# Scores stacked through DRAM, and the attention gate moved onto weight tiles

## The chip, the cores and the metric

One core of a Trainium2 chip runs the kernel. The metric is the device time of one execution in microseconds (us). The engines are TensorE (PE in the rows; its weight loads are PEld), VectorE (DVE), ScalarE (ACT), GpSimd (POOL) and SyncE (SP, which only starts transfers).

## The reference, cut to what matters

Two layers of a diffusion backbone run on 256 latent and 256 context tokens of width 1024. In each, the modulated input is projected to three attention groups; their heads are joined and go through one output projection, whose result is multiplied by a gate of the conditioning before it is added to the stream; a gated convolutional feed-forward follows. The second layer gives only latent tokens out, so there only latent queries are computed.

```python
s = einsum('bhqcd,bhkcd->bhcqk', q, k) * scale      # A: 6 heads, 2 maps each, 32 dimensions
p = softmax(s); p = p[:, :, 0] - lam * p[:, :, 1]

s_win = q @ k_window * scale + bias, masked          # B: 6 heads of 64 dimensions, 8x16 window
p = softmax(concat(s_win, q @ k_ctx * scale))        #    and all context keys

mix = concat(o_a, o_b, o_c) @ w_out                  # C: 4 heads of 96 dimensions
x = layernorm(ALPHA * x + ga * mix) * g + b          # ga: the gate, one number a column
```

## The kernel before

Nearly all products run on numbers split in two, a high part that TensorE's float32r format holds and the rest: hi·hi + lo·hi + hi·lo, three matmuls for one (lines 134 to 136 add them up). ScalarE makes the high part (L121 for weights, L126 and L130 for activations), VectorE the low part by a subtraction (L122, L127, L131).

Tokens stand side by side, 512 columns in layer 0 (256 context, then 256 latent) and, for queries, 256 in layer 1. One projection `fm` gives 128 rows by up to 512 columns, from 24 matmuls. An A tile i holds two heads of two maps of 32 rows; a B tile two heads of 64 rows. Their splits lie in tiles `stq` and `stk`, planes hi and lo beside each other. `score3` (L622) makes a score bank of 128 queries by 256 or 512 keys from three matmuls on 32 rows (A) or 64 (B) of TensorE; it fills two banks in turn, the two maps of a head (A) or the two heads (B), each on its own rows. C's scores (L831) take 96 rows in plain float32, one matmul each. The softmax takes a maximum (L381) and a reciprocal (L385) on VectorE and an exponential on ScalarE (L384); in A the second map is scaled (L702) and joined with the first (L703); then p is transposed (L392) and multiplied with the values (L400). In B, GpSimd masks a bias (L743, L744) that VectorE adds to the score (L745).

The parts of a layer are written in the order of `ORDERS`: "aq1" projects the queries of A's tile 1, "bk2" the keys of B's tile 2, "A0" is the attention of A's tile 0, "W3" the early part of the output projection for one weight block. A list scheduler then sets the order of each engine's own queue when the program is built, from its own planned times; it interleaves projections with attention. Each engine works its queue strictly in that order. Score tiles are slots of a pool: nine "st" in layer 0, seven "stq" and eight "stk" in layer 1; a writer waits for the last reader of its slot.

Weights come by SyncE's transfers into four "raw" buffers. At the end of layer 1's attention the last block of the output projection is added, `gated` (L892) multiplies each of four sums of 128x512 by the gate row on VectorE (L897) and adds it to the stream (L898); normalisation (L318 to L344) and the feed-forward follow.

Of the kernel before, what the change touches and what calls it, by code (L numbers as in the profile page):

```python
# [8 lines left out]
F32 = mybir.dt.float32  # L9
F32R = mybir.dt.float32r  # L10
AF = mybir.ActivationFunctionType
ALU = mybir.AluOpType
# [13 lines left out]
A_SCALE = 32 ** -0.5  # L26
# [4 lines left out]
ROT = [16 * (i // 16) + (i % 16 + 8) % 16 for i in range(32)]  # L31


CORE = (("qf",), ("vm",), ("sq",), ("pT",), ("rpb",), ("p1",), ("rot",),
        ("cosk", "sink", "bones", "ones", "m01", "mneg"), ("st", "stq", "stk"), ("p0",), ("vt",))


# [40 lines left out]
def build(nc, tc, st, I, out):  # L78
    P = 128
# [23 lines left out]
    def scp():  # L103
        return bank("sc", 2)
# [4 lines left out]
    def load(dst, src):  # L109
        nc.sync.dma_start(out=dst, in_=src)  # L110
# [1 line left out]
    def wraw(n):  # L112
        return wp.tile([P, n], F32, tag="raw", name="raw", bufs=4)

    def wsplit(src, n, pl=None, tag="", bufs=3, ring=False):
        raw = pl.tile([P, n], F32, tag="raw" + tag, name="raw", bufs=1) if pl and bufs == 1 and not ring else wraw(n)
        load(raw, src)
        pl = pl or wp
        hi = pl.tile([P, n], F32R, tag="whi" + tag, name="whi", bufs=bufs)
        lo = pl.tile([P, n], F32R, tag="wlo" + tag, name="wlo", bufs=bufs)  # L120
        S.copy(hi, raw)  # L121
        V.tensor_tensor(lo, raw, hi.bitcast(F32), ALU.subtract)  # L122
        return hi, lo

    def split_from(src, hi, lo):
        S.copy(hi, src)  # L126
        V.tensor_tensor(lo, src, hi.bitcast(F32), ALU.subtract)  # L127

    def split_scaled(src, hi, lo, scale):
        S.mul(hi, src, scale)  # L130
        V.scalar_tensor_tensor(lo, src, scale, hi.bitcast(F32), ALU.mult, ALU.subtract)  # L131
# [157 lines left out]
    def gate_row(l, r, cond, j, slot):  # L289
        t = tmp.tile([P, 512], F32, tag=("bada", "adarow")[slot], name="gate", bufs=1)  # L290
        load(t, garow[l, r][cond, 512 * j:512 * j + 512].partition_broadcast(P))
        return t
# [243 lines left out]
    for l in range(L):  # L536
# [82 lines left out]
            pump(PF)  # L619
            return proj(w, [LAT, CTX] if cc["early"] and cols == ALL else [cols])  # L620

        def score3(banks, q, k, rows, r0, qs, nk):  # L622
            for t, (a, b) in enumerate(((0, 0), (0, 1), (1, 0))):
                for n, sc in enumerate(banks):
                    r = slice(r0 + rows * n, r0 + rows * n + rows)
                    T.matmul(sc[:, 0:nk], lhsT=q[r, a, qs], rhs=k[r, b, 0:nk], start=t == 0, stop=t == 2,  # L626
                             tile_position=(r.start, 0))

        def st_q(dt=F32R):
            return ap.tile([P, 2, nq], dt, tag="stq" if last else "st", name="stq", bufs=7 if last else 9)  # L630

        def st_k(dt=F32R):
            return ap.tile([P, 2, 512], dt, tag="stk" if last else "st", name="stk", bufs=8 if last else 9)
# [45 lines left out]
        def proj_aq(i):  # L679
            po = fm(i, qc)  # L680
            q = ap.tile([P, 512], F32, tag="qf", name="qf", bufs=2)
            rope(ap, q[:, LAT], po, 0, P, K["cosk"], K["sink"])
            if not last:
                S.copy(q[:, CTX], po[:, CTX])
            aqs[i] = st_q()
            split_scaled(q[:, qc], aqs[i][:, 0, :], aqs[i][:, 1, :], A_SCALE)

        def proj_ak(i):
            po = fm(3 + i, ALL)
            k = ap.tile([P, 512], F32, tag="qf", name="kf", bufs=2)  # L690
            rope(ap, k[:, LAT], po, 0, P, K["cosk"], K["sink"])
            S.copy(k[:, CTX], po[:, CTX])
            aks[i] = st_k()
            split_from(k, aks[i][:, 0, :], aks[i][:, 1, :])

        def attn_a(i):
            def sco(h, e, qs, qt, nk, name):
                banks = [scp() for _ in range(2)]
                score3(banks, aqs[i], aks[i], 32, 64 * e, qs, nk)
                (p0, s0), (p1, s1) = [softmax_rows(sc, nk, ap, f"p{m}") for m, sc in enumerate(banks)]  # L700
                V.tensor_tensor(s1[:, 1:2], s1[:, 1:2], lam[:, 2:3], ALU.mult)
                V.tensor_scalar_mul(p1[:, 0:nk], p1[:, 0:nk], s1[:, 1:2])  # L702
                V.scalar_tensor_tensor(p0[:, 0:nk], p0[:, 0:nk], s0[:, 1:2], p1[:, 0:nk], ALU.mult, ALU.add)  # L703
                return p0

            def fin(po, c):
                sq = ap.tile([P, 256], F32, tag="sq", name="sq", bufs=2)
                S.activation(sq, po, AF.Square)
                pm = tpp()
                T.matmul(pm[:, 0:256], lhsT=K["bones"], rhs=sq, start=True, stop=True)  # L710
                S.activation(sq, pm[:, 0:256], AF.Ln, bias=epsc)
                S.activation(sq, sq, AF.Exp, scale=-0.5)
                V.scalar_tensor_tensor(sq, po, nw[:, 0:1], sq, ALU.mult, ALU.mult)
                split_from(sq, mix[0][:, i, c], mix[1][:, i, c])

            heads(i, sco, vt, 0, fin)
# [2 lines left out]

        def proj_bq(i):  # L720
            po = fm(6 + i, qc)
            bqs[i] = st_q()
            split_scaled(po[:, qc], bqs[i][:, 0, :], bqs[i][:, 1, :], B_SCALE)

        def proj_bk(i):
            po = fm(9 + i, ALL)
            bks[i] = st_k()
            split_from(po, bks[i][:, 0, :], bks[i][:, 1, :])

        def attn_b(i):  # L730
            banks = []

            def sco(h, e, qs, qt, nk, name):
                if e == 0:
                    banks[:] = [scp() for _ in range(2)]
                    score3(banks, bqs[i], bks[i], 64, 0, qs, nk)
                sc = banks[e]
                if name == "lat":
                    bt = ap.tile([P, 256], F32, tag="rpb", name="rpb", bufs=3)
                    load(bt, I["rpb"][l, h, qt])  # L740
                    b3 = bt.rearrange("p (a c) -> p a c", c=64)
                    with tc.issue_after(hT["pow"]):
                        G.tensor_tensor(b3, b3, K["m01"].unsqueeze(1).to_broadcast([P, 4, 64]), ALU.mult)  # L743
                    G.tensor_tensor(b3, b3, K["mneg"].unsqueeze(1).to_broadcast([P, 4, 64]), ALU.add)  # L744
                    V.tensor_tensor(sc[:, LAT], sc[:, LAT], bt, ALU.add)  # L745
                return normed(sc, nk)

            heads(i, sco, vt, 416 if i else 384, simple_fin(3 + i))
# [88 lines left out]
            pend.extend([ada(l, "b"), ada(l, "c")])  # L837
        outp = {}
        odone = []

        def out_mm(po, t, jb, w, kk, done):
            j = 2 * jb + kk
# [3 lines left out]
                not done and kk == 0, len(done) == 3 and kk == 1)  # L846

        def out_early(jb):
            for hf in range(2 if last else 1):
                w = wsplit(I["w_out"][l, hf, jb], 1024)  # L850
                for t in toks:
                    if not odone:
                        outp[t, hf] = acc() if len(outp) < 3 else adap()
                for kk in range(2):
                    for t in toks:
                        out_mm(outp[t, hf], t, jb, w, kk, odone)
            odone.append(jb)
# [34 lines left out]
        def gated(gates, po, t, hf):  # L892
            c = slice(512 * hf, 512 * hf + 512)
            if hf == 0:
                rsum[t] = sm.tile([P, 4], F32, tag="rsum", name="rsum")
                V.memset(rsum[t][:, 3:4], 0.0)
            V.tensor_tensor(po, po, gates[1 if t < 2 else 0], ALU.mult)  # L897
            V.scalar_tensor_tensor(xr[t][:, c], xr[t][:, c], ALPHA, po, ALU.mult, ALU.add,  # L898
                                   accum_out=rsum[t][:, hf:hf + 1])

# [34 lines left out]
        def token_major(pl, rnd, name, order, act, off, wpl, nres, head, tail, allres=False, nkeep=0):  # L935
# [16 lines left out]
            if allres:  # L952
                rem = [jb for jb in order if jb not in odone]
                ws = {}
                for i, jb in enumerate(rem):
                    for hf in range(2):
                        ws[jb, hf] = wsplit(I[name][l, hf, jb], 1024, wpl if i else None, f"r{hf}" if i else "", 1 if i else 3,
                                            True)
                gts = [gate_row(l, rnd, 0, hf, hf) for hf in range(2)]
                for t in toks:  # L960
                    for i, jb in enumerate(rem):
                        for hf in range(2):
                            for kk in range(2):
                                out_mm(outp[t, hf], t, jb, ws[jb, hf], kk, odone + rem[:i])
                            if i == len(rem) - 1:
                                gated([gts[hf]], outp[t, hf], t, hf)
                    head(t)
                tail(toks)
                return
# [310 lines left out]
```

## Time and profile before

| | us |
|---|---|
| median of 3 runs (1155.33 to 1157.75) | 1156.91 |
| profiled execution, its own time | 1158.58 |
| its span, first to last instruction | 1156.5 |
| TensorE busy in the span | 1107.0 |
| VectorE busy | 836.1 |
| ScalarE busy | 591.2 |
| GpSimd busy | 83.8 |

The mean granted clock of TensorE was 0.986 of full speed. A busy time counts an engine's instructions; matmuls are pipelined, so the duration of one is longer than the step from one to the next. The chain of waits, followed back from the end, tells that step. The profile's chain lies on TensorE for 85% of the span.

### The profile page before, as it was taken

The numbers are of one execution on the slowest core, as the hardware profiler recorded it, in microseconds if no ns is written. First come the engines' busy times: TensorE is split into PE (matmuls) and PEld (weight loads), VectorE is DVE, ScalarE is ACT, GpSimd is POOL, SyncE is SP. The second block draws the span as 40 slices with busy tenths as digits, with TensorE's granted clock in tenths as the row PEclk, the third lists the DMA queues.
The fourth block names the chain that finished last, engine by engine and source line by source line (L and its number), as shares of the span: only waits on it lengthen the run. The fifth ranks groups of instructions, "written<-read, shape, count | busy, mean of one in ns | idle before, by whom it ended". The sixth has DMA issues, their size and how long they took to land.

```text
span 1156.5 us, 17907 instructions
## 1 busy us (share of the span) xinstructions
PE 1107.0 (96%) x6776; PEld 902.1 (78%) x6776; DVE 836.1 (72%) x1505; ACT 591.2 (51%) x1063; POOL 83.8 (7%) x104
## 2 busy tenths in 40 slices
PE   5999999999998999999999999999999979999997
PEld 3877666686778888887888877897778758999985
DVE  4544677757588887986977687666766777888755
ACT  4345556656548644444352245555555656666541
POOL 0000100003123000000000002110000420000000
PEclk9999999999999999999999999998999988999999
DMA  9767112112143554643558894533111333555662
GB/s 362 295 241 279 58 37 74 37 37 86 51 164 97 197 169 144 199 152 116 186 174 309 311 328 131 176 94 99 53 55 56 128 132 121 183 183 188 201 203 89
DMA packets 58213, 179.19 MB, mean 155 GB/s; under 512 B 7024, under 2 KB 12432, under 8 KB 58128
## 3 DMA queue, kind: packets, MB, share of 16 engines
q1 hardware_dynamic: 58128, 178.05, 45.8%
q8 instruction: 54, 0.88, 0.3%
q14 instruction: 31, 0.25, 0.1%
HBM read 176.94 MB, written 1.08 MB: 154 GB/s over the span
## 4 chain that ended last, share of the span: by engine, by line
PE 85%; DVE 6%; ACT 2%; issue 2%; POOL 2%; DMA 2%; SPq 0%; DVEq 0%; POOLq 0%; ACTq 0%
PE acc L134 21%; PE acc L135 21%; PE acc L136 21%; PE sc L626 6%; PE tp L392 3%; PE tp L400 3%; PE sc L831 2%; DVE wlo L122 1%; PE sc L134 1%; PE sc L135 1%; PE sc L136 1%; POOL xn L344 1%; DMA rawr<-in_w_ada_e 1%; PE ada L234 1%; PE ada L136 1%
## 5 line engine op out<-in xcount | busy, mean ns | idle before, releaser
L121 ACT CAST whi<-raw 128x1024 fp32r<-128x1024 f32 (+3 forms) x204 | 212.0, 1043 | 248.7 <-PE acc L135 124.4
L122 DVE TENSOR_TENSOR wlo<-raw,whi 128x1024 fp32r<-128x1024 f32 (+3 forms) x204 | 248.4, 1221 | 121.4 <-ACT whi L121 117.1
L134 PE MATMUL acc<-hhi,whi 128*128 128x256 f32 (+1 forms) x960 | 327.3, 341 | 3.5 <-ACT hhi L360 3.5
L135 PE MATMUL acc<-hlo,whi 128*128 128x256 f32 (+1 forms) x960 | 325.4, 339 | 0.5 <-DVE hlo L361 0.3
L136 PE MATMUL acc<-hhi,wlo 128*128 128x256 f32 (+1 forms) x960 | 324.1, 338 | 0.4 <-DVE wlo L122 0.4
L134 PEld LDWEIGHTS acc<-hhi,whi 128*128 128x128 f32 x960 | 184.7, 193 | 28.2 <-issue 5.4
L135 PEld LDWEIGHTS acc<-hlo,whi 128*128 128x128 f32 x960 | 184.9, 193 | 22.2 <-issue 3.6
L136 PEld LDWEIGHTS acc<-hhi,wlo 128*128 128x128 f32 x960 | 184.6, 192 | 22.1 <-issue 3.8
L384 ACT ACTIVATE p<-sc,nm 128x512 f32<-128x512 f32 (+1 forms) x132 | 81.4, 619 | 26.0 <-DVE nm L381 24.5
L381 DVE TENSOR_REDUCE nm<-sc 128x1 f32<-128x512 f32 (+1 forms) x132 | 77.3, 598 | 22.7 <-PE sc L626 15.9
L393 ACT COPY pT<-tp 128x512 f32<-128x512 f32 (+1 forms) x96 | 49.4, 516 | 56.2 <-PE tp L392 55.8
L626 PE MATMUL sc<-stk,stq 32*128 32x512 f32 (+3 forms) x324 | 75.0, 392 | 1.0 <-ACT p L384 0.9
L626 PEld LDWEIGHTS sc<-stk,stq 32*128 32x128 f32 (+1 forms) x324 | 41.6, 183 | 26.4 <-issue 11.5
L1064 ACT ACTIVATE u<-acc,conv 128x256 f32<-128x256 f32 (+1 forms) x94 | 60.8, 647 | 1.4 <-PE acc L136 1.3
L1067 DVE SCALAR_TENSOR_TENSOR u<-acc,conv,u 128x255 f32<-128x255 f32 (+1 forms) x94 | 55.1, 586 | 6.3 <-ACT u L1064 6.3
L1068 DVE SCALAR_TENSOR_TENSOR u<-acc,conv,u 128x255 f32<-128x255 f32 (+1 forms) x94 | 55.4, 589 | 2.3
L215 DVE SCALAR_TENSOR_TENSOR ac<-raw,scT,ac 128x1024 f32<-128x1024 f32 x42 | 53.4, 1281 | 4.7 <-DMA raw<-in_w_ada 4.6
L392 PE MATMUL tp<-ident,p 128*128 128x128 f32 x320 | 52.6, 279 | 0.6 <-DVE p L674 0.5
L392 PEld LDWEIGHTS tp<-ident,p 128*128 128x128 f32 x320 | 36.8, 140 | 20.8 <-issue 8.5
L134 PE MATMUL acc<-whi,gBhi 128*128 128x512 f32 x133 | 52.0, 392 | 0.0
L135 PE MATMUL acc<-wlo,gBhi 128*128 128x512 f32 x133 | 51.9, 390 | 0.0
L136 PE MATMUL acc<-whi,gBlo 128*128 128x512 f32 x133 | 51.8, 391 | 0.0
(282 smaller groups left out, 1816.6 us busy)
## 6 DMA issues: line engine op xcount, KB each, us to landing
raw<-in_w_up SPq DMA_DIRECT2D x94, 512.0 KB
raw<-in_w_down SPq DMA_DIRECT2D x53, 512.0 KB
adalo<-in_w_ada SPq DMA_DIRECT2D x32, 512.0 KB
raw<-in_w_f SPq DMA_DIRECT2D x27, 512.0 KB
rawr<-in_w_ada SPq DMA_DIRECT2D x24, 512.0 KB
raw<-in_w_ada SPq DMA_DIRECT2D x24, 512.0 KB
raw<-in_w_out SPq DMA_DIRECT2D x16, 512.0 KB
rawr<-in_w_ada_e SPq DMA_DIRECT2D x12, 512.0 KB
```

Source lines behind the costliest of these rows:

```text
L121: S.copy(hi, raw)
L122: V.tensor_tensor(lo, raw, hi.bitcast(F32), ALU.subtract)
L134: T.matmul(o, lhsT=lh, rhs=rh, start=first, stop=False)
L135: T.matmul(o, lhsT=lh, rhs=rl, start=False, stop=False)
L136: return T.matmul(o, lhsT=ll, rhs=rh, start=False, stop=last).ins
L381: V.reduce_max(nm, sc[:, 0:nk], axis=AX.X, negate=True)
L384: hT["exp"] = S.activation(p[:, 0:nk], sc[:, 0:nk], AF.Exp, bias=nm, accum_out=sums[:, 0:1]).ins
L392: T.transpose(pt[:, 128 * kc:128 * kc + 128], p[:, 128 * kc:128 * kc + 128], ident)
L626: T.matmul(sc[:, 0:nk], lhsT=q[r, a, qs], rhs=k[r, b, 0:nk], start=t == 0, stop=t == 2, tile_position=(r.start, 0))
L1064: S.activation(t, po[:, c], AF.Identity, scale=cw[:, 1:2], bias=cw[:, 3:4])
L1067: V.scalar_tensor_tensor(t3[:, :, 1:], p3[:, :, 0:255], cw[:, 0:1], t3[:, :, 1:], ALU.mult, ALU.add)
L1068: V.scalar_tensor_tensor(t3[:, :, 0:255], p3[:, :, 1:], cw[:, 2:3], t3[:, :, 0:255], ALU.mult, ALU.add)
```

## The change

First, A's and B's scores. A projection's split goes into a new tile "hl", of which there is one buffer. `stage` writes its planes to DRAM from GpSimd's queue, in an order in which the hi and lo planes lie above one another: hi, lo, hi for queries and hi, hi, lo for A's keys, hi, lo for B's keys. Further transfers on the same queue read stacked tiles back, 96 rows for A (three planes of 32) and 128 for B. A map's score is then one matmul of 96 rows; a B head's is two of 128, on (hi, lo) and then (lo, hi) of the query against (hi, lo) of the key. That is 144 score matmuls for 324. Of A's tile i there are now two query and two key tiles (one a head), of B's two query tiles; the slots stay as many. GpSimd starts 108 transfers, 54 a layer.

Second, the gate of layer 1. `wsplit` multiplies each of the eight 128x1024 weight tiles of its output projection by the gate rows on VectorE (L120 after) before ScalarE and VectorE split them; the four multiplications of the sums are gone.

```diff
-CORE = (("qf",), ("vm",), ...
+CORE = (("qf",), ("hl",), ("vm",), ...
...
-    def wsplit(src, n, pl=None, tag="", bufs=3, ring=False):
+    def wsplit(src, n, pl=None, tag="", bufs=3, ring=False, gate=None):
...
         load(raw, src)
+        if gate is not None:
+            r3 = raw.rearrange("p (k c) -> p k c", k=2)
+            V.tensor_tensor(r3, r3, gate.unsqueeze(1).to_broadcast([P, 2, 512]), ALU.mult)
...
-        def score3(banks, q, k, rows, r0, qs, nk):
...
+        def hl_tile(n):
+            return ap.tile([P, 2, n], F32R, tag="hl", name="hl", bufs=1)
+
+        def stage(hl, n, heads, order, name):
+            p = P // heads
+            d = dp.tile([heads, len(order), p, n], F32, tag=name, name=name, bufs=2)
+            for s, w in enumerate(order):
+                G.dma_start(d[:, s], hl[:, w, :].bitcast(F32))
+            return d
...
-            aqs[i] = st_q()
-            split_scaled(q[:, qc], aqs[i][:, 0, :], aqs[i][:, 1, :], A_SCALE)
+            hq = hl_tile(nq)
+            split_scaled(q[:, qc], hq[:, 0, :], hq[:, 1, :], A_SCALE)
+            dq = stage(hq, nq, 4, (0, 1, 0), "daq")
+            for e in range(2):
+                q = st_q()
+                vq = dq[2 * e:2 * e + 2].rearrange("m s p t -> (s p) m t").bitcast(F32R)
+                G.dma_start(q[0:96], vq)
+                aqs[2 * i + e] = q
...
-                banks = [scp() for _ in range(2)]
-                score3(banks, aqs[i], aks[i], 32, 64 * e, qs, nk)
+                for m in range(2):
+                    sc = scp()
+                    T.matmul(sc[:, 0:nk], lhsT=aqs[h][0:96, m, qs], rhs=aks[h][0:96, m, 0:nk], start=True, stop=True)
+                    pq.append(softmax_rows(sc, nk, ap, f"p{m}"))
...
+            dq = stage(hq, nq, 2, (0, 1, 0), "dbq")
+            vq = dq.rearrange("m s p t -> (s p) m t").bitcast(F32R)
+            bqs[i] = [st_q() for _ in range(2)]
+            for a in range(2):
+                G.dma_start(bqs[i][a], vq[64 * a:64 * a + 128])
...
+            dk = stage(hk, 512, 2, (0, 1), "dbk")
             bks[i] = st_k()
+            G.dma_start(bks[i], dk.rearrange("m s p t -> (s p) m t").bitcast(F32R))
...
-                    score3(banks, bqs[i], bks[i], 64, 0, qs, nk)
+                for a in range(2):
+                    T.matmul(sc[:, 0:nk], lhsT=bqs[i][a][:, e, qs], rhs=bks[i][:, e, 0:nk],
+                             start=(a == 0), stop=(a == 1))
...
+            if last and not gts:
+                gts.extend(gate_row(l, "b", 0, hf, hf) for hf in range(2))
...
-                w = wsplit(I["w_out"][l, hf, jb], 1024)
+                w = wsplit(I["w_out"][l, hf, jb], 1024, gate=gts[hf] if last else None)
...
-            V.tensor_tensor(po, po, gates[1 if t < 2 else 0], ALU.mult)
+            if gates:
+                V.tensor_tensor(po, po, gates[1 if t < 2 else 0], ALU.mult)
...
-                                gated([gts[hf]], outp[t, hf], t, hf)
+                                gated(None, outp[t, hf], t, hf)
```

On TensorE in layer 0, at the second A attention (A1), the order of before has the three matmuls of a map between matmuls of a projection (acc) and transposes (tp).

```order
620 L626 MATMUL sc<-stk,stq 128x512 x3
621 L135 MATMUL acc<-hlo,whi 128x512
622 L392 MATMUL tp<-ident,p 128x128 x4
623 L626 MATMUL sc<-stk,stq 128x512 x3
624 L136 MATMUL acc<-hhi,wlo 128x512
625 L134 MATMUL acc<-hhi,whi 128x512
626 L135 MATMUL acc<-hlo,whi 128x512
627 L626 MATMUL sc<-stk,stq 128x512 x3
```

The changed kernel has, in the same attention, one matmul a map, its lines numbered anew.

```order
629 L719 MATMUL sc<-stk,stq 128x512
630 L138 MATMUL acc<-hlo,whi 128x512
631 L139 MATMUL acc<-hhi,wlo 128x512
632 L137 MATMUL acc<-hhi,whi 128x512
633 L138 MATMUL acc<-hlo,whi 128x512
634 L719 MATMUL sc<-stk,stq 128x512
635 L395 MATMUL tp<-ident,p 128x128 x2
636 L403 MATMUL tp<-pT,vt 64x128 x8
```

A group of three has become one matmul on 96 rows, and the plain matmuls between the maps are the same kind.

GpSimd's queue before holds, behind C's key copies, only the bias work of B.

```order
8 L795 COPY stk<-stk 32x512 x3
9 L743 TENSOR_TENSOR rpb<-rpb,m_716 128x256
10 L744 TENSOR_TENSOR rpb<-rpb,mneg 128x256
11 L743 TENSOR_TENSOR rpb<-rpb,m_716 128x256
12 L744 TENSOR_TENSOR rpb<-rpb,mneg 128x256
```

After, the transfers of layer 0's twelve projections stand there; daq, dak, dbq and dbk are the DRAM tiles, and this piece runs from the keys of A's tile 0 to those of its tile 2.

```order
19 L632 DMA dak<-hl 4x32x512 x3
20 L711 DMA stk<-dak 96x2x512
21 L632 DMA daq<-hl 4x32x512 x3
22 L711 DMA stk<-dak 96x2x512
23 L697 DMA stq<-daq 96x2x512
24 L632 DMA daq<-hl 4x32x512 x3
25 L632 DMA dbk<-hl 2x64x512 x2
26 L697 DMA stq<-daq 96x2x512 x3
27 L757 DMA stk<-dbk 128x2x512
28 L632 DMA dak<-hl 4x32x512 x3
29 L632 DMA dbk<-hl 2x64x512 x2
```

A read (stk or stq) waits for the writes of its DRAM tile and for a slot, and the next projection's writes stand behind it in the same queue.

On VectorE at the end of layer 1's output projection the order of before goes from the last split to a multiplication by the gate.

```order
1066 L127 TENSOR_TENSOR mixlo<-tp,mixhi 128x256
1067 L897 TENSOR_TENSOR acc<-acc,gate 128x512
1068 L898 SCALAR_TENSOR_TENSOR xr_3507,rsum<-xr_3507,acc 128x512
1069 L897 TENSOR_TENSOR acc<-acc,gate 128x512
1070 L898 SCALAR_TENSOR_TENSOR xr_3507,rsum<-xr_3507,acc 128x512
```

After, it goes straight to the addition to the stream.

```order
1102 L130 TENSOR_TENSOR mixlo<-tp,mixhi 128x256
1103 L929 SCALAR_TENSOR_TENSOR xr_3478,rsum<-xr_3478,acc 128x512 x2
1104 L321 TENSOR_SCALAR mv<-rsum 128x1
1105 L957 SCALAR_TENSOR_TENSOR pn<-xr_3478,mv,ln_g 128x1024
1106 L929 SCALAR_TENSOR_TENSOR xr_3480,rsum<-xr_3480,acc 128x512
```

The multiplications now stand further up, one for each weight tile, five of the eight ahead of layer 1's first bias addition.

## Rows read from the trace of the kernel before

**Rows 1.** Page, busy time of each engine (share of the span) and instructions.

```profile
PE 1107.0 (96%) x6776; PEld 902.1 (78%) x6776; DVE 836.1 (72%) x1505; ACT 591.2 (51%) x1063; POOL 83.8 (7%) x104
```

**Rows 2.** Windows: length; busy PE, PEld, DVE, ACT, POOL (count); PEclk; DMA share; GB/s.

```profile
155.00:262.00 107.00, 107.00 (x634) 76.94 (x633) 77.32 (x210) 63.26 (x166) 0.00 (x0) 1.00 0.14 45
262.00:330.00 68.00, 66.64 (x437) 48.47 (x436) 50.28 (x114) 38.55 (x93) 14.48 (x18) 1.00 0.33 107
820.00:890.00 70.00, 69.68 (x440) 53.09 (x440) 49.01 (x111) 38.73 (x88) 0.00 (x0) 1.00 0.16 55
890.00:945.00 55.00, 53.40 (x360) 40.26 (x359) 38.64 (x75) 30.76 (x58) 14.80 (x18) 1.00 0.39 130
```

**Rows 3.** The same windows, score matmuls of line 626 alone: busy PE and PEld.

```profile
155.00:262.00 107.00, 32.79 (x146) 19.31 (x148) 1.00 0.14 45
262.00:330.00 68.00, 13.92 (x72) 7.81 (x70) 1.00 0.33 107
820.00:890.00 70.00, 18.99 (x72) 9.85 (x72) 1.00 0.16 55
890.00:945.00 55.00, 9.35 (x36) 4.62 (x36) 1.00 0.39 130
```

**Rows 4.** Chain of waits around A's and C's scores: start, us, what.

```profile
147.41 0.86 PE sc L831 x2
148.27 0.23 PE acc L134
...
196.09 0.23 PE acc L135
...
196.79 0.89 PE sc L626 x3
197.68 0.43 PE acc L135
...
831.02 0.12 PE acc L136
```

**Rows 5.** Window of the longest stretch with TensorE full.

```profile
400.00:700.00 300.00, 298.84 (x1371) 242.41 (x1371) 238.73 (x276) 118.07 (x144) 0.00 (x0) 1.00 0.62 208
```

**Rows 6.** Groups by line and form: count, busy us, mean ns, idle before.

```profile
L122 DVE TENSOR_TENSOR wlo<-raw,whi 128x1024 fp32r<-128x1024 f32 x196 | 241.0, 1233 | 119.1 <-ACT whi L121 114.8 <-PE sc L626 2.2 <-DMA ln_b<-in_ln_b 1.7
L702 DVE TENSOR_SCALAR p<-p,sums 128x512 f32<-128x512 f32 x24 | 11.6, 483 | 0.5
```

**Rows 7.** Chain of waits, where a transfer ended a wait.

```profile
263.29 3.42 DMA rpb<-in_rpb
...
380.38 6.62 DMA raw<-in_w_ada
```

**Rows 8.** Timeline of ScalarE, splits of A and B projections: start, us, what.

```profile
100.18 0.63 ACT L130 ACTIVATE stq<-qf 128x512 fp32r<-128x512 f32 x1 [1.44 <-DVE qf L377]
...
251.09 0.59 ACT L130 ACTIVATE stq<-acc 128x512 fp32r<-128x512 f32 x1
...
797.07 0.42 ACT L130 ACTIVATE stq<-qf 128x256 fp32r<-128x256 f32 x1 [1.63 <-DVE qf L377]
...
813.84 0.42 ACT L130 ACTIVATE stq<-qf 128x256 fp32r<-128x256 f32 x1
...
885.86 0.40 ACT L130 ACTIVATE stq<-acc 128x256 fp32r<-128x256 f32 x1
```

**Rows 9.** Window in which TensorE paused in layer 1.

```profile
784.00:796.00 12.00, 10.75 (x45) 8.74 (x46) 7.33 (x16) 7.49 (x16) 2.63 (x3) 0.72 0.30 87
```

**Rows 10.** Chain of waits behind layer 1's output projection.

```profile
939.64 0.71 DVE acc L897
...
945.01 0.62 DVE ada L897
945.65 0.71 DVE xr L898 x2
```

**Rows 11.** Timeline of TensorE, last matmul of that projection.

```profile
943.07 0.39 PE L136 MATMUL ada<-whi,mixlo 128*128 128x512 f32 x1
```

More of the change, by code (lines that the diff above doesn't have):

```diff
@@ L31 @@
 ROT = [16 * (i // 16) + (i % 16 + 8) % 16 for i in range(32)]
-CORE = (("qf",), ("vm",), ("sq",), ("pT",), ("rpb",), ("p1",), ("rot",),
+CORE = (("qf",), ("hl",), ("vm",), ("sq",), ("pT",), ("rpb",), ("p1",), ("rot",),
         ("cosk", "sink", "bones", "ones", "m01", "mneg"), ("st", "stq", "stk"), ("p0",), ("vt",))
@@ L620, in fm @@
             return proj(w, [LAT, CTX] if cc["early"] and cols == ALL else [cols])
-        def score3(banks, q, k, rows, r0, qs, nk):
[L623 to L627, printed above, removed]
+        def hl_tile(n):
[6 more added lines that the diff above has]
+            return d
         def st_q(dt=F32R):
@@ L692, in proj_ak @@
             S.copy(k[:, CTX], po[:, CTX])
-            aks[i] = st_k()
-            split_from(k, aks[i][:, 0, :], aks[i][:, 1, :])
+            hk = hl_tile(512)
+            split_from(k, hk[:, 0, :], hk[:, 1, :])
+            dk = stage(hk, 512, 4, (0, 0, 1), "dak")
+            for e in range(2):
+                k = st_k()
+                vk = dk[2 * e:2 * e + 2].rearrange("m s p t -> (s p) m t").bitcast(F32R)
+                G.dma_start(k[0:96], vk)
+                aks[2 * i + e] = k
         def attn_a(i):
             def sco(h, e, qs, qt, nk, name):
-                banks = [scp() for _ in range(2)]
-                score3(banks, aqs[i], aks[i], 32, 64 * e, qs, nk)
-                (p0, s0), (p1, s1) = [softmax_rows(sc, nk, ap, f"p{m}") for m, sc in enumerate(banks)]
+                pq = []
+                for m in range(2):
+                    sc = scp()
+                    T.matmul(sc[:, 0:nk], lhsT=aqs[h][0:96, m, qs], rhs=aks[h][0:96, m, 0:nk], start=True, stop=True)
+                    pq.append(softmax_rows(sc, nk, ap, f"p{m}"))
+                (p0, s0), (p1, s1) = pq
                 V.tensor_tensor(s1[:, 1:2], s1[:, 1:2], lam[:, 2:3], ALU.mult)
@@ L721, in proj_bq @@
             po = fm(6 + i, qc)
-            bqs[i] = st_q()
-            split_scaled(po[:, qc], bqs[i][:, 0, :], bqs[i][:, 1, :], B_SCALE)
+            hq = hl_tile(nq)
+            split_scaled(po[:, qc], hq[:, 0, :], hq[:, 1, :], B_SCALE)
+            dq = stage(hq, nq, 2, (0, 1, 0), "dbq")
[3 more added lines that the diff above has]
+                G.dma_start(bqs[i][a], vq[64 * a:64 * a + 128])
         def proj_bk(i):
             po = fm(9 + i, ALL)
+            hk = hl_tile(512)
+            split_from(po, hk[:, 0, :], hk[:, 1, :])
+            dk = stage(hk, 512, 2, (0, 1), "dbk")
             bks[i] = st_k()
-            split_from(po, bks[i][:, 0, :], bks[i][:, 1, :])
+            G.dma_start(bks[i], dk.rearrange("m s p t -> (s p) m t").bitcast(F32R))
         def attn_b(i):
-            banks = []
             def sco(h, e, qs, qt, nk, name):
-                if e == 0:
-                    banks[:] = [scp() for _ in range(2)]
-                    score3(banks, bqs[i], bks[i], 64, 0, qs, nk)
-                sc = banks[e]
+                sc = scp()
+                for a in range(2):
+                    T.matmul(sc[:, 0:nk], lhsT=bqs[i][a][:, e, qs], rhs=bks[i][:, e, 0:nk],
+                             start=(a == 0), stop=(a == 1))
                 if name == "lat":
@@ L839, in build @@
         odone = []
+        gts = []
         def out_mm(po, t, jb, w, kk, done):
@@ L957, in token_major @@
                         ws[jb, hf] = wsplit(I[name][l, hf, jb], 1024, wpl if i else None, f"r{hf}" if i else "", 1 if i else 3,
-                                            True)
-                gts = [gate_row(l, rnd, 0, hf, hf) for hf in range(2)]
+                                            True, gts[hf])
                 for t in toks:
```

## The prediction

> **What bounds the kernel now.** I read the busy totals first. TensorE is busy 96% of the span, VectorE 72%, ScalarE 51%, GpSimd 7% [rows 1]; so time is won where TensorE gets less to do, as long as VectorE can follow. Next I cut the two attention parts out of both layers: 155 to 262 us is mostly A of layer 0, 262 to 330 B of layer 0, 820 to 890 A of layer 1, 890 to 945 B of layer 1 [rows 2]. The reader is to see TensorE full in each (107.0 of 107, 66.6 of 68, 69.7 of 70, 53.4 of 55) and VectorE at 70 to 74% (77.3, 50.3, 49.0, 38.6 us). The same windows restricted to the score line give what the scores hold of TensorE: 32.8, 13.9, 19.0 and 9.4 us, 75.0 together [rows 3]. The chain of waits shows what one score costs [rows 4]: the three matmuls of one map take 0.89 us, and the plain matmul behind them 0.43 where others take 0.23. So every group costs 0.20 us more than it shows. In those four stretches the chain holds 42, 16, 18 and 10 such groups.
>
> **Part 1, the score matmuls.** A unit is two maps of one query tile (A) or two heads of one tile (B), six matmuls before. There are 36 units in A (layer 0 12 at 512 and 12 at 256 columns, layer 1 12 at 512) and 18 in B (6, 6 and 6). Removed is the time of [rows 3] plus 0.20 us a group: layer 0 A 32.8 + 8.4 = 41.2 us, B 13.9 + 3.2 = 17.1, layer 1 A 19.0 + 3.6 = 22.6, B 9.4 + 2.0 = 11.4. Added are plain matmuls, 2 a unit in A and 4 in B, at 0.23 us for 512 columns and 0.12 for 256 [rows 4]: 8.4, 8.4, 5.5 and 5.5 us. I charge no 0.20 us to the new ones: the C scores already use 96 rows, and the matmul behind two of them takes 0.23 [rows 4]. TensorE's need thus falls by 32.8, 8.7, 17.1 and 5.9 us, 64 in all.
>
> That is not the gain, for VectorE's work does not shrink. The longest stretch in which TensorE was full (298.8 of 300 us) had VectorE at 80%, 238.7 us [rows 5]; nothing here shows it higher with TensorE full. In layer 0's A TensorE would need 74.2 us and VectorE 77.3. I take 85% as what VectorE reaches when both are near full, and 80 and 100% as the ends. Layer 0 A: 77.3/0.85 = 91, saves 16 (10 to 30). Layer 0 B: 50.3/0.85 = 59.2, TensorE's own 57.9 and 1.4 of waits give the same, saves 8.7 (5 to 8.7). Layer 1 A gets five of the new gate multiplies ahead of the first bias addition, at the 1.23 us of the same shape and engine [rows 6]: 49.0 + 6.2 = 55.2, /0.85 = 65, saves 5 (1 to 15). Layer 1 B gets three: 38.6 + 3.7 = 42.3, /0.85 = 49.8, saves 5 (2 to 5.9). Sum 35 us, 18 to 60.
>
> On B the Trainium skill argues the other way. "TensorE: Matmul & The Clock Gate", Part 3 "Packing small matmuls", says that row-tiled matmuls on different rows run concurrently; six in two row tiles would then last three, 0.69 us at 512 columns, while four plain ones last 0.92. By it B would lose 2 us in layer 0 and 1.4 in layer 1, and without the 14 us of B the sum below would be −14. The rows here do not bear it out: B's units hold 13.9/12 = 1.16 and 9.4/6 = 1.56 us even before the 0.20 us [rows 3], since the two banks seldom come free together.
>
> **Part 2, the trip through DRAM.** Each of 24 projections now ends in 2 or 3 writes and 1 or 2 reads on GpSimd's queue, 108 DMAs where it had none. Neither their issue nor their landing is in any row. Nearest are SyncE's: a 128 KB load kept GpSimd waiting 3.42 us of its flight, a 512 KB one ScalarE 6.62 us [rows 7]. The new ones move 128 to 512 KB, so 3.4 to 6.6 us each way, and I take 4: issue, write, read make about 9 us from split to usable tile, and the next split may start once the writes are down, after some 6 (5 to 9). The whole effect lies between nothing and rival (c); it cannot be negative, as no wait leaves.
>
> Mostly this is covered: a projection stands one or two parts ahead of its attention, and the twelve splits of a layer are 9 to 14 us apart in the mean [rows 8]. It is not in three kinds of place. First, the buffer of the split is single. In layer 1 four splits stand 16.8 us apart from first to last [rows 8], 5.6 each, against 6: each adds up to 1 us, and as exponentials stand behind the split on ScalarE, TensorE's transposes wait with them. Second, reads into score slots wait for scores of an earlier attention. In layer 0 the second tile of aq1 and the first of ak2 can be fetched only after A0's and A1's first-half scores, with about 5.5 and 4.3 us of other TensorE work before they are needed: 0 to 2.3 us late each. Third, such a read blocks the one GpSimd queue, so later projections' writes, and through the buffer ScalarE, wait behind it; on SyncE the convolution and norm rows of layer 1 wait for writes too, with weight loads behind them. I allow 6 us for all. TensorE's granted clock adds to that: in a stretch of 12 us where TensorE was idle for 1.25 us it averaged 0.72 [rows 9], 12 x 0.28 = 3.4 us lost. One such fall: 3. So part 2 costs 9 us, 0 to 20 in my case.
>
> The Trainium skill has prices: "DMA: Bandwidth & Descriptors", section "Anatomy of one DMA", gives 2.0 us plus bytes/436e3 for a GpSimd-issued DMA. That is an estimate of 2.6 and 2.9 us for 256 and 393 KB, by which part 2 would come to some 5 us; no run here shows it.
>
> **Part 3, the gate.** Four L897, the first of 0.71 and the last of 0.62 us, leave the end of layer 1's output projection, all on the chain [rows 10]. The last matmul begins at 943.07 and lasts 0.39 [rows 11], so the last residual addition of 0.7 us cannot end before 944.2 instead of 946.4: at most 2.2 us, and what is late next is the variance pass on ScalarE, GpSimd and the norm, in series as before. I take 2 (1 to 2.2). The multiplies' cost on VectorE is in part 1; they precede ScalarE's cast of a weight block, which four buffers let run ahead.
>
> **Sum.** −35 − 2 + 9 = −28. The profiled execution took 1158.6 us, 1.7 more than the median: 1130.6, or **1129** against the median.
>
> **Rivals.** (a) VectorE is no limit and the trips are hidden. For it: much of VectorE's work is weight splitting, which can be shifted. −60 − 2 gives 1095, to 1118 with half of the VectorE limit and a few us of trips. (b) VectorE stays at 80%, −18 − 2, and the trips cost 9: 1146; with 14, 1151. For it: 80% is all that was seen. A variant comes from a rule. A fast VectorE operation could hold GpSimd off while it writes a DMA; the scaling of a map takes 0.48 us [rows 6], and if each of five DMAs of a stage waits half of one, 1.2 us for some eight tight stages add 10 us to my case: 1139. "SBUF — State Buffer", section "SBUF: two separate sides", of the Trainium skill has this rule ("DVE blocks DMA") for GpSimd-issued DMAs; with its 3.1 us for 0.62 a stage would be slower by 12 us and rival (c) decide; no row before shows it. (c) Slower: the staging queue becomes the bound. From aq0 of layer 0 to its last split there are 151 us for 11 gaps, and in layer 1 89 us for the ten behind its second [rows 8], 13.7 and 8.9 us each. If a stage holds the queue and the buffer longer than that, every stage hands its excess to ScalarE and TensorE. It decides from about 12.3 us a stage: (12.3 − 8.9) × 11 = 37, the whole gain. At 14, (0.3 + 5.1) × 11 = 59 less 37 is +22: 1179. For it: one queue in order, with waits for slots in it. Against: two flights at 4 us make 9. That the scores are not stacked can be left out: the TensorE order holds 144 score matmuls where there were 324.
>
> **Chances.** Forecast, 1120 to 1142: 0.42. (a) 0.18. (b) and above it to 1154: 0.20. Within 0.2% (2.3 us, about what a measurement of this kernel can tell from no change): 0.05, (b) with more late reads. (c) 0.15. Faster is 0.42 + 0.18 + 0.20 = 0.80. The range 1106 to 1160 leaves out a third of (a) and most of (c).
>
> **What would show it.** Right: the score line near 28 us of TensorE instead of 75 and no 0.43 us behind it; VectorE over 80% in 155 to 245 us; layer 0's A some 16 us shorter; first transpose after layer 1's projection 2 us closer to the last matmul. Wrong: waits of ScalarE's splits (hl) for DMA above 15 us in sum, TensorE idle before scores with a DMA into stq or stk as releaser, or a clock below 0.98 in A. If TensorE is full and VectorE at 95%, (a) was right.

## The result, and the profile after

The changed kernel takes 1218.68 us (median of 4 runs), the kernel before 1157.33 beside it: the ratio is 1.0558 (1.054 to 1.0576), 5.6% slower. The forecast was 1129, faster; 1218.68 lies outside the range. What happened is rival (c), and it cost more than rival (c) was priced at.

The page first: busy times, DMA queues, and the chain's shares by engine.

```profile
PE 1090.6 (89%) x6596; PEld 902.7 (74%) x6596; DVE 833.2 (68%) x1509; ACT 587.5 (48%) x1063; POOL 163.6 (13%) x212
...
q1 hardware_dynamic: 58128, 178.05, 43.6%
q0 software_dynamic: 32064, 31.23, 11.5%
...
PE 60%; DMA 14%; DVE 7%; issue 5%; POOL 3%; ACT 2%; DVEq 0%; ACTq 0%; POOLq 0%
```

TensorE has less to do, 1090.6 us of busy time for 1107.0 [rows 1], and is busy 89% of a longer span. There is a new queue (q0, GpSimd's transfers, 31 MB), and the chain that was TensorE's is DMA for 14%.

The windows of the four attention parts, which end at about the same events as those of [rows 2] (first addition of a bias, end of B, last matmul of layer 1's output projection).

```profile
155.00:285.00 130.00, 104.01 (x615) 80.48 (x616) 81.45 (x231) 68.39 (x185) 26.61 (x36) 0.89 0.53 127
285.00:350.00 65.00, 63.56 (x415) 47.80 (x414) 48.70 (x115) 38.90 (x93) 13.86 (x18) 1.00 0.42 142
860.00:960.00 100.00, 71.31 (x393) 58.47 (x392) 50.45 (x114) 38.42 (x87) 22.05 (x29) 0.83 0.42 109
960.00:1012.00 52.00, 51.39 (x354) 40.20 (x352) 43.12 (x80) 31.55 (x60) 17.97 (x20) 1.00 0.54 166
```

TensorE is no longer full in the A parts: 104.0 of 130 us and 71.3 of 100, where it was 107.0 of 107 and 69.7 of 70. Both B windows are full and 3 us shorter. VectorE is at 63 and 50% in A, so it is not the limit. The granted clock, 1.00 in [rows 2], is 0.89 and 0.83 here.

The chain of waits around one projection of layer 0 shows what fills the gaps: start, length, what.

```profile
150.49 0.63 ACT hl L129
...
152.14 0.71 POOL dak L632
152.84 10.97 DMA dak<-hl
...
164.00 0.64 ACT hl L133
```

ScalarE splits a projection at 150.49; the last of its three writes goes out by 152.84 and needs 10.97 us to land; only then may ScalarE split the next one, 13.5 us after the split before. The same step stands in layer 0's chain at 118.08 (10.94 us) and 187.31 (10.88), and for B's keys at 224.30 (12.81). Where several of these follow one another, TensorE has nothing at all:

```profile
830.00:840.00 10.00, 0.00 (x0) 0.00 (x0) 0.81 (x2) 1.46 (x4) 0.98 (x2) 0.58 0.28 76
```

The DMA view gives the median from issue to landing, the last number of a row.

```profile
dak<-hl POOLq DMA_DIRECT2D x18, 256.0 KB, 9.5
...
stk<-dak POOLq DMA_DIRECT2D x12, 384.0 KB, 4.6
...
dbk<-hl POOLq DMA_DIRECT2D x12, 256.0 KB, 11.3
...
daq<-hl POOLq DMA_DIRECT2D x9, 256.0 KB, 8.9
...
dbq<-hl POOLq DMA_DIRECT2D x9, 256.0 KB, 11.0
```

Writes of 256 KB take 9 to 11 us, reads of 384 KB 4.6 (A's queries, not shown, 6.3). The nearest rows had been 3.42 us for 128 KB and 6.62 for 512 [rows 7]. The waits name the same place: waiting engine, line, what for, us in total, times, longest.

```profile
POOL stk L711 <- DMA dak<-hl: 49.4, 5, 12.9
...
PEld sc L719 <- ACT p L387: 44.3, 25, 8.6
...
ACT hl L133 <- DMA dak<-hl: 31.8, 4, 10.4
...
ACT hl L133 <- DMA dbk<-hl: 20.5, 3, 9.8
```

The first transpose after layer 1's output projection did come closer to the last matmul, in TensorE's timeline: 7.3 us from start to start, 9.0 before (from 943.07 of [rows 11] to 952.05).

```profile
1011.28 0.39 PE L139 MATMUL ada<-whi,mixlo 128*128 128x512 f32 x1
...
1018.55 1.97 PE L350 MATMUL tp<-ident,xn 128*128 128x128 f32 x8 [6.88 <-POOL xn L347]
```

When the events come, in us from the start of each profiled span ("part 1" is the change without its trips, "planes" and "planes, 2 buffers" two kernels of the experiments):

| | before | after | part 1 | planes | planes, 2 buffers |
|---|---|---|---|---|---|
| first bias addition, layer 0 (end of A) | 262.8 | 286.2 | 241.4 | 249.8 | 244.0 |
| first addition to the stream, layer 0 (end of B) | 321.5 | 341.3 | 294.5 | 302.6 | 298.9 |
| first bias addition, layer 1 | 896.5 | 967.0 | 854.5 | 871.5 | 865.7 |
| last matmul of its output projection | 943.1 | 1011.3 | 898.2 | 921.0 | 909.7 |
| span | 1156.5 | 1222.6 | 1109.9 | 1132.8 | 1120.8 |

Layer 0's A part loses 23 us and layer 1's 51 (70.5 less the 19.8 of layer 0); both B parts gain 2 to 4, and the end gains 2.

### The profile page after: what moved, and what is told of

The parts are those of the page before. It is cut to its first block, busy times and chain, and to the rows that moved or that the text cites. A ratio compares the mean times of both kernels' runs of the same rounds, so it can differ in the third digit from the quotient of the medians.

```text
span 1222.6 us, 17813 instructions
## 1 busy us (share of the span) xinstructions
PE 1090.6 (89%) x6596; PEld 902.7 (74%) x6596; DVE 833.2 (68%) x1509; ACT 587.5 (48%) x1063; POOL 163.6 (13%) x212
## 2 busy tenths in 40 slices
DMA packets 90278, 210.41 MB, mean 172 GB/s; under 512 B 26224, under 2 KB 34320, under 8 KB 90192
## 4 chain that ended last, share of the span: by engine, by line
PE 60%; DMA 14%; DVE 7%; issue 5%; POOL 3%; ACT 2%; DVEq 0%; ACTq 0%; POOLq 0%
PE acc L137 16%; PE acc L139 16%; PE acc L138 16%; DMA dak<-hl 5%; DMA dbk<-hl 4%; DMA dbq<-hl 2%; PE tp L403 2%; PE tp L395 2%; DMA daq<-hl 2%; PE sc L763 1%; DVE wlo L125 1%; PE sc L858 1%; POOL xn L347 1%; DMA raw<-in_w_out 1%; POOL rs L325 1%
## 5 line engine op out<-in xcount | busy, mean ns | idle before, releaser
L137 PEld LDWEIGHTS acc<-hhi,whi 128*128 128x128 f32 x960 | 187.4, 195 | 26.3 <-ACT hhi L363 4.2
L139 PEld LDWEIGHTS acc<-hhi,wlo 128*128 128x128 f32 x960 | 187.1, 195 | 18.3 <-issue 0.3
L395 PE MATMUL tp<-ident,p 128*128 128x128 f32 x320 | 56.6, 296 | 27.1 <-DVE p L680 14.4
L395 PEld LDWEIGHTS tp<-ident,p 128*128 128x128 f32 x320 | 42.2, 153 | 46.8 <-issue 23.2
L325 POOL TENSOR_TENSOR rs<-mv,mhalf 128x1 f32<-128x1 f32 x20 | 15.5, 776 | 427.8 <-DVE mv L323 427.7
L719 PE MATMUL sc<-stk,stq 96*128 96x512 f32 (+1 forms) x72 | 31.5, 444 | 37.3 <-ACT p L387 37.3
```

Of the source, the lines that this page charges most:

```text
L137: T.matmul(o, lhsT=lh, rhs=rh, start=first, stop=False)
L139: return T.matmul(o, lhsT=ll, rhs=rh, start=False, stop=last).ins
L395: T.transpose(pt[:, 128 * kc:128 * kc + 128], p[:, 128 * kc:128 * kc + 128], ident)
```

## The experiments

**The gate alone**, on the kernel before.

```diff
+            V.tensor_tensor(r3, r3, gate.unsqueeze(1).to_broadcast([P, 2, 512]), ALU.mult)
...
-                                gated([gts[hf]], outp[t, hf], t, hf)
+                                gated(None, outp[t, hf], t, hf)
```

> The gate's move alone, on the kernel before; scores as before. If it does what I charged it with: the four multiplications behind the last matmul go, the pause of TensorE there shrinks from 8.6 us to about 6.5, VectorE has room for eight multiplications of 1.2 us, and the time is about 1155 (0.2% faster). Rival: the multiplications delay the low parts of weight tiles in layer 1's B part, TensorE waits there, and the time is 1157 or more.

1156.79 us beside 1155.60; ratio 1.0008 (0.9995 to 1.0021): no change. The end of the projection did what was forecast, in the timeline of TensorE:

```profile
945.27 0.39 PE L139 MATMUL ada<-whi,mixlo 128*128 128x512 f32 x1
...
952.60 1.97 PE L350 MATMUL tp<-ident,xn 128*128 128x128 f32 x8 [6.94 <-POOL xn L347]
```

From the last matmul to the transposes it is 7.3 us instead of 9.0. But that last matmul starts 2.2 us later than in [rows 11]. The chain of waits of layer 1's B part, and VectorE's timeline behind it, show why:

```profile
918.48 3.60 DMA raw<-in_w_out
...
923.32 0.76 DVE sc L748 x2
```

```profile
922.18 1.22 DVE L120 TENSOR_TENSOR raw<-raw,gate 128x1024 f32<-128x1024 f32 x1 [2.05 <-DMA raw<-in_w_out]
```

The gate's multiplication (L120) is now VectorE's first touch of a weight block, so VectorE itself waits for the load: this one starts only at 918.48 and takes 3.60 us, and VectorE stands idle for the last 2.05 of them, with the bias addition of a score (L748) behind the multiplication in its queue. TensorE runs dry for some 2.4 us and its clock falls, in the window of that part:

```profile
893.90:945.70 51.80, 49.34 (x308) 36.51 (x306) 40.04 (x72) 28.57 (x55) 16.92 (x18) 0.93 0.47 145
```

**The stacked scores without the gate** (the changed kernel with the gate's lines taken back).

```diff
-                                gated(None, outp[t, hf], t, hf)
+                                gated([gts[hf]], outp[t, hf], t, hf)
```

> The stacked scores alone, without the gate's move. If the whole loss comes from the stacking and its trips: about 1220, the changed kernel's 1218.7 plus the 2 us of the gate. Rival, the gate rows' early loads and multiplications make things worse together with the trips: 1205 or less.

1222.39 us; ratio 1.059 (1.0574 to 1.0607). The whole loss is the stacking's.

**The stacked matmuls without the trips.** The split goes straight into one score tile, and no transfer is left. This kernel leaves out the stacking itself, so it computes something else; its matmuls have the changed kernel's shapes. A's projections and B's queries fill one score tile instead of two.

```diff
-            hq = hl_tile(nq)
+            hq = st_q()
             split_scaled(q[:, qc], hq[:, 0, :], hq[:, 1, :], A_SCALE)
-            dq = stage(hq, nq, 4, (0, 1, 0), "daq")
...
+            aqs[2 * i] = aqs[2 * i + 1] = hq
```

> The changed kernel without the trip: each split writes straight into one score tile, no transfer is issued, and the scores are the same 144 matmuls of 96 and 128 rows on rows that are not stacked (so the attention's numbers are not the reference's). Theory 'the trip is the loss, the stacked matmuls save what VectorE lets them': 1120, from the 35 + 2 us of the prediction. With no VectorE limit at all: 1095. Rival 'the new score matmuls or their order cost by themselves': 1150 or more. VectorE should be busy 85% between 155 us and the end of layer 0's A part.

1111.54 us; ratio 0.9623 (0.961 to 0.9635), 44 us faster than before. So the stacked matmuls save what part 1 of the prediction says or more, and the trips, with the second tile that they need, cost 1218.7 − 1111.5 = 107 us. The chain of waits in layer 0's A:

```profile
186.04 0.24 PE sc L709
186.28 0.23 PE acc L137
...
189.31 0.23 PE sc L709
```

A map's score is one piece of 0.23 us, and the plain matmul behind it takes 0.23, not the 0.43 of [rows 4]. In the window of that part VectorE reaches 75.87 of 90 us with TensorE full: 84%, where the prediction had taken 85.

```profile
150.00:240.00 90.00, 90.00 (x588) 71.23 (x587) 75.87 (x220) 63.12 (x176) 0.00 (x0) 1.00 0.16 54
```

**Whole planes written, the stacking left to the reads.**

```diff
-            d = dp.tile([heads, len(order), p, n], F32, tag=name, name=name, bufs=2)
-            for s, w in enumerate(order):
-                G.dma_start(d[:, s], hl[:, w, :].bitcast(F32))
+            d = dp.tile([2, P, n], F32, tag=name, name=name, bufs=2)
+            for w in range(2):
+                G.dma_start(d[w], hl[:, w, :].bitcast(F32))
...
-                G.dma_start(q[0:96], vq)
+                for s, w in enumerate((0, 1, 0)):
+                    G.dma_start(q[32 * s:32 * s + 32],
+                                dq[w, 64 * e:64 * e + 64].rearrange("(m p) t -> p m t", m=2).bitcast(F32R))
```

> Same trip, another shape: a split is written as two whole 128-row planes (512 KB a projection of 512 columns instead of 768), and the doubling and stacking are done by more reads of 32 or 64 rows (6 for an A projection instead of 2). Theory 'the writes are slow because of their shape, with 4 or 2 heads as the outermost dimension': they land in 4 to 5 us instead of 9 to 11, and the time falls to 1175 to 1195. Rival 'a write to DRAM from this queue is slow whatever its shape': landing stays near 8 us, time 1205 to 1225. Rival 'the number of DMAs on the queue decides': more of them, so above 1220.

1136.37 us; ratio 0.9831 (0.9807 to 0.9854): the same change, with its transfers shaped otherwise, is 1.7% faster than the kernel before, and 82 us faster than the changed kernel, more than any of the expectations. There are more transfers now (156, 108 before), so their number is not what cost. The DMA view:

```profile
stk<-dak POOLq DMA_DIRECT2D x36, 128.0 KB, 3.0
...
dak<-hl POOLq DMA_DIRECT2D x12, 256.0 KB, 3.5
...
dbk<-hl POOLq DMA_DIRECT2D x12, 256.0 KB, 2.5
...
daq<-hl POOLq DMA_DIRECT2D x6, 256.0 KB, 4.1
```

The same 256 KB land in 2.5 to 4.1 us instead of 9 to 11. But this kernel also writes a third less for A and for B's queries. So:

**The third write put back, in the new shape.**

```diff
-            d = dp.tile([2, P, n], F32, tag=name, name=name, bufs=2)
-            for w in range(2):
-                G.dma_start(d[w], hl[:, w, :].bitcast(F32))
+            d = dp.tile([len(order), P, n], F32, tag=name, name=name, bufs=2)
+            for s, w in enumerate(order):
+                G.dma_start(d[s], hl[:, w, :].bitcast(F32))
```

> As e5_plain, but with the changed kernel's third write back: 768 KB a projection of 512 columns again, in three whole 128-row planes. Theory 'the shape alone was slow': writes land in 3 to 5 us as in e5_plain, and the time is 1135 to 1142. Rival 'the third fewer bytes and writes made e5_plain faster': most of the loss comes back, above 1170.

1135.43 us; ratio 0.9809 (0.9791 to 0.9828). The bytes written are the changed kernel's again and nothing is lost: it is the shape that was slow, not the bytes. The reads stayed cut into pieces of 32 and 64 rows here, so what whole reads would cost beside whole planes is not shown; but the writes' landing falls by 5 to 8 us, and A's key reads land in 2.8 us a piece of 128 KB, 4.6 for 384 KB at once.

```profile
dak<-hl POOLq DMA_DIRECT2D x18, 256.0 KB, 4.2
...
dbk<-hl POOLq DMA_DIRECT2D x12, 256.0 KB, 3.2
```

**The slow shape from another queue.**

```diff
-                G.dma_start(d[:, s], hl[:, w, :].bitcast(F32))
+                S.dma_start(d[:, s], hl[:, w, :].bitcast(F32))
```

> The changed kernel with its writes, shape and all, started from ScalarE's queue; the reads stay on GpSimd's. Theory 'the shape is slow only where GpSimd makes the transfers': writes land in 4 to 5 us, time below 1160. Theory 'the shape is slow on any queue': landing near 10 us, and ScalarE waits as before, 1200 to 1230. ScalarE also waits for VectorE's low parts before it starts their writes, some 1 us a projection.

1276.39 us; ratio 1.1043 (1.1017 to 1.1068): worse still, and beyond what either theory gave; the shape is slow on this queue too. On ScalarE's timeline the next split starts 15.6 us after the first write of the one before, with 11.32 us idle for the landing.

```profile
158.36 1.98 ACTq L632 DMA_DIRECT2D dak<-hl  x3
...
173.98 0.63 ACT L133 ACTIVATE hl<-qf 128x512 fp32r<-128x512 f32 x1 [11.32 <-DMA dak<-hl]
```

Here nothing else hides what the writes use, in windows in which hardly anything but them is moving: DMA share and GB/s are the last two columns. The first window is a B projection's (two heads), the other two an A projection's (four).

```profile
151.00:155.00 4.00, 4.00 (x20) 3.35 (x19) 1.82 (x8) 2.16 (x5) 0.00 (x0) 1.00 0.16 57
170.00:173.00 3.00, 0.00 (x0) 0.00 (x0) 0.00 (x0) 0.00 (x0) 0.00 (x0) 0.50 0.26 100
183.00:187.00 4.00, 4.00 (x43) 2.88 (x42) 1.89 (x6) 2.87 (x10) 0.00 (x0) 1.00 0.26 98
```

Two heads move 57 GB/s, four 98 to 100, at 0.16 and 0.26 of the 16 DMA engines: about 2.5 and 4.2 engines. A write from ScalarE's queue whose outermost dimension is the heads is carried by about as many engines as there are heads. The Trainium skill states such a rule: "DMA: Bandwidth & Descriptors", section "Why a DMA increments its semaphore by 16 and not by 1", says that the engines of a transfer are the largest number up to 16 that divides the slowest dimension of both sides. These windows agree with it, for the writes from ScalarE.

For GpSimd's own writes this is not the whole story. Here is a window of the changed kernel in which hardly anything but the writes of one split moves, and behind it one with the same three writes as whole planes (the kernel with the third write put back).

```profile
153.00:157.00 4.00, 4.00 (x23) 1.94 (x22) 3.15 (x7) 2.47 (x5) 0.54 (x1) 1.00 0.54 51
```

```profile
153.00:154.80 1.80, 1.80 (x13) 0.98 (x12) 1.80 (x5) 1.54 (x4) 0.00 (x0) 1.00 0.93 351
```

In the first, 0.54 of the 16 DMA engines, some 8.6, are busy and move 51 GB/s; in the second 0.93, some 14.9, move 351. So GpSimd's three writes together held more engines than ScalarE's did, and each busy engine moved a quarter of what it moves with whole planes. Beside the data stand many small packets: 298 of 347 are under 512 bytes in the first window, 42 of 195 in the second. That these packets are what slows the writes is not shown; how many engines each single write had, no row shows.

**Two buffers for the split**, slow writes kept.

```diff
-            return ap.tile([P, 2, n], F32R, tag="hl", name="hl", bufs=1)
+            return ap.tile([P, 2, n], F32R, tag="hl", name="hl", bufs=2)
```

> The changed kernel with two buffers for the split instead of one; the slow writes stay. If it is the single buffer through which slow writes stop ScalarE and TensorE: most of the loss goes, 1160 to 1185. If it is the one queue, with reads waiting in it for landings and slots: little changes, 1205 to 1220.

1179.23 us; ratio 1.0202 (1.018 to 1.0224). 40 of the 107 us go, with the writes as slow as before (dak 9.2, dbk 11.7 us in its DMA view). ScalarE's splits wait 18 us for B's writes where two rows of the changed kernel's waits, for A's and B's, have 52; GpSimd's reads still wait:

```profile
POOL stk L711 <- DMA dak<-hl: 35.7, 4, 9.2
...
POOL stq L697 <- DMA daq<-hl: 35.4, 5, 10.2
...
ACT hl L133 <- DMA dbk<-hl: 17.8, 2, 13.4
```

**Copies by GpSimd instead of transfers.**

```diff
-                G.dma_start(d[:, s], hl[:, w, :].bitcast(F32))
+                G.tensor_copy(dst[p * s:p * s + p, m, :], hl[r0 + p * m:r0 + p * m + p, w, :])
```

> No transfers: GpSimd itself copies the pieces of a split into the stacked tiles, 12 copies of 32 rows for an A projection, 8 and 4 of 64 rows in B, at about 0.6 us (a 32x512 copy of GpSimd takes 603 ns in the trace of the changed kernel). A stage is then some 8 us, without landing times. If the stage time decides: between the kernel without trips and e5_plain, 1112 to 1130. Rival 'copies on GpSimd slow VectorE or last longer beside it': above 1136.

1151.09 us; ratio 0.9954 (0.9937 to 0.9972): slower than expected, where the rival put it. The groups by line and form show that a copy takes 0.73 to 0.76 us here, not 0.60, so twelve are a stage of 9 us, in which the buffer stays taken. The 0.60 came from C's six key copies in the changed kernel; the same six take 0.81 us here (the last row) and 0.76 in the kernel before. Whether the longer copies are all of the loss was not tried.

```profile
L630 POOL CAST stk<-hl 32x512 fp32r<-32x512 f32 x72 | 52.4, 728 | 44.3 <-ACT hl L129 15.5 <-PE sc L714 13.8 <-PE sc L852 11.9
...
L630 POOL CAST stq<-hl 32x512 fp32r<-32x512 f32 x36 | 27.4, 762 | 29.5 <-PE sc L714 16.4 <-ACT hl L133 11.7
...
L816 POOL COPY stk<-stk 32x512 f32<-32x512 f32 x6 | 4.6, 805 | 69.2 <-ACT stk L814 69.1
```

**Planes and two buffers.**

```diff
-            return ap.tile([P, 2, n], F32R, tag="hl", name="hl", bufs=1)
+            return ap.tile([P, 2, n], F32R, tag="hl", name="hl", bufs=2)
```

> e5_plain (whole planes written) with two buffers for the split. e5_plain's 1136 stands 25 us above the kernel without trips. If the single buffer still holds those: 1118 to 1128. If it is the queue, the slots and the traffic: 1131 to 1138.

1121.34 us; ratio 0.9686 (0.9658 to 0.9713), the fastest whole version: 3.1% ahead of the kernel before, 10 us above the kernel without trips. With two buffers, whole planes are thus worth 58 us (1179 to 1121); with one, 82. One wait of its chain in layer 0 that the other does not have is for a bias load:

```profile
244.47 10.25 DMA rpb<-in_rpb
```

Whether that wait makes up the 10 us was not tried.

**B back to row-tiled scores**, on planes and two buffers; A stays stacked.

```diff
-                sc = scp()
-                for a in range(2):
-                    T.matmul(sc[:, 0:nk], lhsT=bqs[i][a][:, e, qs], rhs=bks[i][:, e, 0:nk],
-                             start=(a == 0), stop=(a == 1))
+                if e == 0:
+                    banks[:] = [scp() for _ in range(2)]
+                    score3(banks, bqs[i], bks[i], 64, 0, qs, nk)
+                sc = banks[e]
```

> As e10_plain_hl2, but B goes back to the row-tiled scores of the kernel before, without trips: 12 of 24 projections are staged. By the prediction's terms B's stacked scores save 14 us and its trips cost part of the rest: if B's trips are hidden by now, this is 5 to 14 us slower than e10_plain_hl2; if B's trips cost more than its stacking saves, it is faster, 1115 to 1125.

1128.28 us; ratio 0.9738 (0.9707 to 0.9768). By the medians B's stacking with its trips is worth 7 us, though the two intervals just touch. B does not lose by it, as it would if all its row-tiled matmuls ran side by side.

**Planes and two buffers without the gate.**

```diff
-                                gated(None, outp[t, hf], t, hf)
+                                gated([gts[hf]], outp[t, hf], t, hf)
```

> As e10_plain_hl2, without the gate's move. The gate alone gave 1.0008 (0.9995 to 1.0021). If it is neutral here too: within 2 us of e10_plain_hl2. If its 2 us appear where the B part has more room: 2 to 3 us slower.

1122.83 us; ratio 0.9709 (0.9675 to 0.9743), 1.5 us above its twin, with overlapping intervals: no effect of the gate can be told here either.

## Why the prediction was wrong

- **Part 1, the score matmuls: right, and some 10 us too small.** 35 us were forecast with VectorE at 85%; the kernel without trips has it at 84% and gains 44 us with the gate's move in it. By its events layer 0's A saves 21.4 us (16 forecast), B 5.6 (8.7), layer 1's A 15.0 (5) and B 2.9 (5). The term that was too small is layer 1's A. The gate's multiplications lasted 1.20 to 1.23 us each, as charged, but the window priced, 820 to 890, is only a part of that stretch. Here it is whole, before and without trips:

```profile
794.00:896.50 102.50, 102.18 (x640) 78.69 (x639) 69.01 (x157) 55.29 (x118) 0.00 (x0) 1.00 0.19 63
```

```profile
765.00:854.50 89.50, 89.50 (x590) 73.43 (x588) 72.69 (x163) 54.48 (x118) 0.00 (x0) 1.00 0.23 72
```

By the prediction's own rule VectorE's 69.0 us and the gate's 6.2 would make (69.0 + 6.2)/0.85 = 88.5 us (an estimate), 14 us saved; 89.5 and 13 were measured.

- **Part 2, the trip: this is the step that failed.** "The new ones move 128 to 512 KB, so 3.4 to 6.6 us each way, and I take 4." The reads of 384 and 512 KB stayed inside (4.6 to 6.3 us); the writes of 256 KB took 8.9 to 11.3. I bounded them by bytes, from loads of another shape on another queue, and overlooked that the write's outermost dimension is 4 or 2 heads. The third write put back shows that bytes and their number were not it. "After some 6 (5 to 9)" for the next split was thus 13.5, beyond the 12.3 from which rival (c) decides. Range and chances were built on the 6. Two of the prediction's own signs of being wrong came: ScalarE's splits waited 52 us for transfers in two rows alone (sign: 15 in sum), and the clock was 0.89 and 0.83 in A (sign: below 0.98).
- **The places were named rightly, at the wrong size.** The single buffer with ScalarE behind it: 40 of 107 us go with a second one. The queue with its reads: in the kernel with two buffers GpSimd's reads still wait for landings, and with the writes as whole planes 58 of the other 67 us go too. Slots: by the waits of the changed kernel GpSimd's reads wait some 49 us for scores and transposes of earlier parts, and 125 us for landings; what the slots cost by themselves no run separates.
- **Rival (c)** had the mechanism and +22 us at 14 us a stage; +61 came. Its formula handed on only what a stage exceeds the mean gap by. In layer 0 a stage of 13.5 us does not exceed the mean gap of 13.7, so by the formula nothing would be lost there; yet its A part is 45 us longer than without trips (286.2 − 241.4). Splits come in bunches, so a mean gap hides less than it seems to. It left out the clock as well: at a mean of 0.952 instead of 0.986, 1222.6 x 0.048 − 1156.5 x 0.014 = 42 us more of clock are lost (an estimate), part of them while TensorE had nothing to do anyway.
- **Part 3, the gate: right at its place, wrong in sum.** The end is 1.7 us shorter (2 forecast) and the time the same, since "four buffers let run ahead" did not hold: VectorE stands idle for up to 2.05 us for a weight block that is still in flight.
- **VectorE holding off GpSimd's transfers** (the variant in rival (b)): GpSimd's issues took 0.66 to 0.84 us in the mean. Landing, not issue, was long, and VectorE does not account for it: in the window from 830 to 840 us, into which most of one such landing falls (13.0 us by the chain), VectorE works 0.81 us of 10, and whole planes moved 351 GB/s with VectorE busy throughout.

## What to carry to other kernels

A transfer's time is not read from its bytes alone: look at its outermost dimension first, and try a layout in which both sides have many rows there, even if that takes more transfers (here the same bytes written as whole planes, with smaller reads, are worth 83 us, 7%). A new hop between a producer and its consumer is priced by how long it keeps the producer's buffer, against the shortest gaps between its uses and not the mean; two buffers cost 4 KB a partition and gave back 40 us. An edit that moves work from the end of a stage to the arrival of its inputs can make its engine wait for the load, with all that is queued behind.

## What the runs showed of the hardware that was not expected

- A write of 256 KB from GpSimd's queue with 4 or 2 heads outermost landed in 9 to 11 us, one with 128 rows outermost in 2.5 to 4.2; from ScalarE's queue such writes moved 57 GB/s with two heads and 98 to 100 with four.
- The changed kernel's transfers broke into 26224 packets under 512 bytes, the kernel with three whole planes 9808, the changed kernel with its writes on ScalarE's queue 7900, the kernel before 7024 (the lines on packets of the profile's pages). So most of the small packets come with GpSimd's writes of that shape, and with neither the shape on ScalarE's queue nor whole planes on GpSimd's. What they do is not shown.
- The same copy of 32 rows of 512 by GpSimd took 0.60 us in the changed kernel, 0.76 in the kernel before and 0.81 in the kernel in which GpSimd makes all the copies.
